# Routing of the second mixture beside its first expert products, mixture weights in transfers of 2 MB, and another order of the first transfers

## The chip, the cores and the metric

One core of a Trainium2 chip runs the whole program in one launch. The metric is device time in microseconds (us). Arrays are float32; some TensorE operands are in the type that the rows call fp32r, and a value is then carried as a high and a low part (names ending in h and l).

## The reference, cut to what matters

Two fused transformer blocks work on 256 tokens of width 1024. The first one has attention and a mixture of 32 experts (hidden width 512, two experts a token). The second one has two layers: a mixer each, then a dense feed-forward of width 2816 in the first layer and a mixture of 8 experts of that width, two a token, in the second, and a gated per-layer projection after each. This is the order of what is computed:

```python
x = x + ((g_gla * y_gla + g_att * y_att) @ w_out[l]).astype(x.dtype)      # first block
x = x + hier_moe(rms_norm(x, norm2_g[l]), w_router_group[l], ...)         # 32 experts
...
for i in range(DEPTH_2):                                                  # second block
    ...
    h = h + jnp.concatenate([y_a, y_b, y_c], axis=-1) @ w_out[i]
    hn = rms_norm_2(h, g_ffn[i])
    if i % 2 == 0:
        f = swiglu(hn, ffn_w1[j], ffn_w3[j], ffn_w2[j])
    else:
        f = moe_swiglu(hn, router_w[j], router_b[j], moe_w1[j], moe_w3[j], moe_w2[j])
    h = h + f
    gate = jax.nn.sigmoid(rms_norm_2(h, g_ple[i]) @ ple_gate_w[i])
    h = h + (p[i] @ ple_proj_w[i]) * gate
```

A mixture's expert computes `(silu(x @ w_gate[e]) * (x @ w_up[e])) @ w_down[e]` for the tokens that its router sends to it.

## The kernel before, in words

The phases run one after the other: b1 (the first block's attention), moe1 (the first mixture), mix0, ffn0, ple0, mix1, ffn1 (the second mixture, function `moe2`), ple1, and fin. Activations stay on the chip; weights are streamed.

**The stream (class `Stream`, lines 236 to 275).** `plan` (L525) lists all weight tiles of the program in the order of use, each [128, 2048] float32, 1 MB, or less. `fill` issues their loads on SP's queue (L264) as long as a buffer is free: one of three in the base ring, which any phase may use, or one of a wider pool that lives as long as its phase (`WIDE`, L23: 13 for moe1, 6 for ffn1). `get` hands out the next tile and frees the one handed out before. A phase's wide pool may be opened while the phase ahead still runs, and its loads start then.

**The start (`run`, L554).** x is loaded in two transfers on SP's queue, behind it the first three weight tiles; the vectors pv and the constants c0 come on ScalarE's queue, and the router table sm1 on GpSimd's. `block1` (L649) loads the constants c1, which the decay of the attention reads, and the smaller a2 on GpSimd's queue. The first products on TensorE are sums over the squares of x.

**The first mixture.** 128 tiles of gate and up weights (wgu) and 64 of down weights (wdn) come through the ring; the tokens of each expert are gathered by a product with a one-hot matrix.

**The second mixture (`moe2`, L1894).** The eight experts go in two halves c of four. In each half, 11 groups j make 256 hidden columns of the gate and up products: `first_products` (L1930) takes eight tiles k, and for each one calls `tiles` (L1918), which issues 16 matmuls with 32-column weights (two row blocks), copies three 512-column pieces of the tile to `fw` (picked by registers), and issues 12 matmuls from them for a third block, which is shared by the three fuller experts of four. The group's products are scaled by `rsl`, go through Silu and a multiplication into `ft`, and are transposed into `hT` beside the next group (`later`, `flush`). Then two times d of 22 tiles make the down products, evicted with the gate weights `wsl` into `ys`/`yf`, which `combine` sends back to the tokens by products with `pt`.

**Its routing.** In a pool m2r that is closed after the first group: logits, the two best experts (`top2`), the places of the tokens (`places`), the one-hot `P` (`base`: 64 places for each of four experts; `more`: 12 blocks of 32 further places, from the strips `px`), and the expert of each half that has fewest tokens (`fewest`). `gather(0)` makes the first half's inputs, eight gathers of 4 matmuls by column block, each two beside a tile of the first group. `of_slots` makes `rsl` by one-column sums. `rest()` is a generator with the remaining routing: the one-hot and the eight gathers of the second half, `of_slots` for it, the gate weights (`shares`), the transposes of P into `pt`, the products of P with the weights whose one-column sums make `wsl`, and the flag of the overflow. It is put into a queue at the first group's k = 3, and three of its steps are taken at each tile from there; what is left is drained after the group.

**The overflow.** If an expert has more tokens than places, a branch (`overflow`, L976) computes these again without limits. It stands behind group j = 5 of the first half, and its buffer xs lies in the last columns of hT.

**The order of the work.** The program is written in the order of the code, and a planner with costs of its own then orders the instructions of each engine; it does so for each stretch between branches by itself. Each engine and each queue then runs its list in order, and semaphores hold an instruction until its inputs are there.

## Time and profile before

| what | value |
|---|---|
| time, median of 3 runs | 2163.77 us (2163.45 to 2166.29) |
| the profiled execution | 2167.51 us, of which the span is 2165.9 us |
| granted TensorE clock, mean of the span | 0.976 |
| busy: PE, PEld | 2016.7 us (93%), 1461.7 us (67%) |
| busy: DVE, ACT, POOL | 1060.6 us (49%), 1080.2 us (50%), 18.7 us (1%) |
| DMA | 613.73 MB in 88665 packets, mean 283 GB/s |
| loads w<-wgu, w<-wdn, w<-m | 128, 64 and 264 of 1024 KB, 19.9, 19.9 and 10.7 us to landing |

PE is TensorE's matmuls, PEld its weight loads beside them, DVE VectorE, ACT ScalarE, POOL GpSimd, and SP issues loads alone. L230 is the one line that issues every matmul. A row names tiles as out<-in; in brackets stands the idle time before it and what ended it. The span in 40 slices of 54 us, each digit a tenth of the slice:

```profile
PE   7999998787877779999999999999899999999997
PEld 6999994222222248879999888866566756666746
PEclk9999999899999999999999999889999999999998
DMA  5344597999999983316555331449999999999981
```

The first mixture is in the slices 7 to 15, the second one in the slices 26 to 39.

### The profile page before, as it was taken

The numbers are of one execution on the slowest core, as the hardware profiler recorded it, in microseconds if no ns is written. First come the engines' busy times: TensorE is split into PE (matmuls) and PEld (weight loads), VectorE is DVE, ScalarE is ACT, GpSimd is POOL, SyncE is SP. The second block draws the span as 40 slices with busy tenths as digits, with TensorE's granted clock in tenths as the row PEclk, the third lists the DMA queues.
The fourth block names the chain that finished last, engine by engine and source line by source line (L and its number), as shares of the span: only waits on it lengthen the run. The fifth ranks groups of instructions, "written<-read, shape, count | busy, mean of one in ns | idle before, by whom it ended". The sixth has DMA issues, their size and how long they took to land. (4 is left out here: it accounts for less than half of the span.)

```text
span 2165.9 us, 44126 instructions
## 1 busy us (share of the span) xinstructions
PE 2016.7 (93%) x17740; PEld 1461.7 (67%) x17740; DVE 1060.6 (49%) x2809; ACT 1080.2 (50%) x2178; POOL 18.7 (1%) x29
## 2 busy tenths in 40 slices
PE   7999998787877779999999999999899999999997
PEld 6999994222222248879999888866566756666746
DVE  5787653100100037777666787536655115566115
ACT  5566642000000025456456735457677777777775
POOL 0000000000000010000000100000000000000000
PEclk9999999899999999999999999889999999999998
DMA  5344597999999983316555331449999999999981
GB/s 179 120 146 149 175 376 305 418 420 420 419 420 420 419 343 109 109 61 216 179 193 191 114 128 52 175 159 396 399 410 418 416 405 407 418 418 417 418 351 47
DMA packets 88665, 613.73 MB, mean 283 GB/s; under 512 B 9879, under 2 KB 12071, under 8 KB 18560
## 3 DMA queue, kind: packets, MB, share of 16 engines
q1 hardware_dynamic: 86272, 604.74, 71.1%
q0 software_dynamic: 1344, 5.10, 0.7%
q8 instruction: 143, 2.34, 0.4%
q10 hardware_dynamic: 832, 0.94, 0.1%
q14 instruction: 74, 0.61, 0.1%
HBM read 609.69 MB, written 1.05 MB: 282 GB/s over the span
## 5 line engine op out<-in xcount | busy, mean ns | idle before, releaser
L314 ACT COPY fw<-w 128x512 f32 x792 | 439.0, 617 | 137.3 <-ACT fw L314 91.9
L341 ACT CAST wh<-w 128x512 fp32r<-128x512 f32 (+2 forms) x500 | 289.8, 585 | 293.8 <-PE ps L230 247.1
L342 DVE TENSOR_TENSOR wl<-w,wh 128x512 fp32r<-128x512 f32 (+2 forms) x500 | 317.9, 646 | 169.9 <-ACT wh L341 161.8
L230 PE MATMUL ps<-w,hT 128*32 128x512 f32 x1920 | 311.0, 597 | 31.4 <-DMA w<-wdn 26.0
L230 PE MATMUL ps<-rawh,wh 128*128 128x256 f32 x960 | 277.4, 289 | 1.1 <-ACT rawh L341 1.1
L230 PE MATMUL ps<-rawl,wh 128*128 128x256 f32 x960 | 271.0, 282 | 0.5 <-DVE rawl L342 0.5
L230 PE MATMUL ps<-rawh,wl 128*128 128x256 f32 x960 | 270.5, 282 | 0.0
L230 PE MATMUL ps<-fw,xg 128*32 128x384 f32 (+2 forms) x2112 | 252.8, 382 | 0.0
L230 PE MATMUL ps<-w,xg 128*32 128x512 f32 x1024 | 199.5, 600 | 43.2 <-DMA w<-wgu 43.0
L2093 DVE STREAM_TRANSPOSE hT<-ft 32x64 f32<-32x64 f32 x968 | 228.3, 236 | 16.3 <-DVEq L985 0.7
L230 PE MATMUL ps<-w,rawh 128*32 128x512 f32 x1408 | 206.2, 607 | 6.4 <-issue 6.4
L230 PE MATMUL ps<-w,rawl 128*32 128x512 f32 x1408 | 211.7, 593 | 0.0
L230 PEld LDWEIGHTS ps<-w,hT 128*32 128x32 f32 x1920 | 116.8, 110 | 135.6 <-DMA w<-wdn 64.0
L230 PEld LDWEIGHTS ps<-fw,xg 128*32 128x32 f32 x2112 | 137.8, 110 | 83.0 <-issue 24.0
L230 PEld LDWEIGHTS ps<-rawh,wh 128*128 128x128 f32 x960 | 181.8, 190 | 5.1 <-ACT rawh L341 1.6
L230 PEld LDWEIGHTS ps<-rawl,wh 128*128 128x128 f32 x960 | 181.9, 190 | 1.9 <-DVE rawl L342 0.7
L230 PEld LDWEIGHTS ps<-rawh,wl 128*128 128x128 f32 x960 | 181.9, 189 | 1.5 <-issue 0.9
L230 PEld LDWEIGHTS ps<-w,xg 128*32 128x32 f32 x1024 | 42.1, 109 | 185.7 <-DMA w<-wgu 111.7
L230 PEld LDWEIGHTS ps<-w,rawl 128*32 128x32 f32 x1408 | 105.2, 110 | 34.4 <-issue 0.9
L230 PE MATMUL ps<-hh,wh 128*128 128x256 f32 x416 | 124.4, 300 | 0.1
L230 PE MATMUL ps<-fw,hT 128*32 128x128 f32 (+2 forms) x1056 | 121.1, 380 | 0.5 <-ACT fw L314 0.3
L230 PE MATMUL ps<-hh,wl 128*128 128x256 f32 x416 | 116.2, 281 | 0.2 <-DVE wl L342 0.2
(520 smaller groups left out, 2983.7 us busy)
## 6 DMA issues: line engine op xcount, KB each, us to landing
w<-m SPq DMA_DIRECT2D x264, 1024.0 KB, 10.7
w<-wgu SPq DMA_DIRECT2D x128, 1024.0 KB, 19.9
w<-wdn SPq DMA_DIRECT2D x64, 1024.0 KB, 19.9
w<-f SPq DMA_DIRECT2D x32, 1024.0 KB, 5.1
w<-wz SPq DMA_DIRECT2D x20, 1024.0 KB, 5.5
w<-wdh SPq DMA_DIRECT2D x24, 768.0 KB, 4.3
w<-wb SPq DMA_DIRECT2D x16, 1024.0 KB, 5.6
w<-wo SPq DMA_DIRECT2D x8, 1024.0 KB, 5.1
```

The source lines that it names most:

```text
L230: return self.k.nc.tensor.matmul(out, lhsT, rhs, start=new, stop=stop, skip_group_check=True, **kw)
L314: self.nc.scalar.copy(out, in_)
L341: self.nc.scalar.copy(h, src)
L342: self.nc.vector.tensor_sub(l, src, h.bitcast(F32))
L2093: nc.vector.transpose(hT[32 * f:32 * f + 32, 2 * j:2 * j + 2, o:o + 32], ts[r][32 * s:32 * s + 32, 64 * q:64 * q + 64].rearrange("p (i d) ...
```

## The change

It has three parts.

The mixtures' weights. Where the wide pool of moe1 or ffn1 has a free buffer, the stream loads two tiles by one transfer of 2 MB into a buffer [128, 4096] (6 such for moe1, 3 for ffn1). Where it has none, the pair goes into two free buffers of the base ring as two transfers of 1 MB. The host arrays m13 and m2 are laid out so that such a pair is one row of 16 KB in each partition.

```diff
-WIDE = {"b1": 0, "moe1": 13, "mix0": 0, "mix1": 0, "ffn0": 2, "ffn1": 6, "ple0": 4, "ple1": 4, "fin": 0}
+WIDE = {"b1": 0, "moe1": 6, "mix0": 0, "mix1": 0, "ffn0": 2, "ffn1": 3, "ple0": 4, "ple1": 4, "fin": 0}
...
-            c = [j for j in range(len(self.pools)) if self.free[j] and (j == 0 or ph == self.phase)]
-            if not c:
+            wide = len(self.pools) > 1 and self.free[1] and ph == self.phase
+            two = ph in ROUTED and not self.issued % 2
+            if two and wide:
+
+                self.free[1] -= 1
+                t = self.pools[1].tile([128, 4096], F32, name="w")
+                self.k.nc.sync.dma_start(t, self.whole[self.issued])
+                self.tiles += [(None, t[:, :2048]), (1, t[:, 2048:])]
+                self.issued += 2
+                continue
+            j = 1 if wide and ph not in ROUTED else 0
+            if self.free[j] < 1 + (two and j == 0):
                 return
-            j = c[-1]
             self.free[j] -= 1
             t = self.pools[j].tile([128, 2048], F32, name="w")
-            self.k.nc.sync.dma_start(t[:, :src.shape[-1]], src)
+
+            n = src.shape[-1] // (1 if self.issued else 4)
+            for c in range(0, src.shape[-1], n):
+                self.k.nc.sync.dma_start(t[:, c:c + n], src[:, c:c + n])
             self.tiles.append((j, t))
             self.issued += 1
...
-                    p += [(ph, A["m2"][c, i, k].rearrange("p e d -> p (e d)")) for i in range(2) for k in range(22)]
-        return p
+                    q += [A["m13"][c, j, k].rearrange("p k e d -> p (k e d)") for j in range(11) for k in range(4)]
+                    q += [A["m2"][c, i, k].rearrange("p k e d -> p (k e d)") for i in range(2) for k in range(11)]
+            for ap in q:
+                if ph in ROUTED:
+                    whole[len(p)] = ap
+                p += [(ph, h) for h in half(ap)]
+        return p, whole
```

The first transfers. x comes in four transfers, the program's first weight tile in four column pieces, and the constants c1 on SP's queue, behind what was issued on it before.

```diff
-            for k in range(0, 8, 4):
-                nc.sync.dma_start(x[:, k:k + 4], A["x"][k:k + 4].rearrange("k p s -> p k s"))
+            for k in range(0, 8, 2):
+                nc.sync.dma_start(x[:, k:k + 2], A["x"][k:k + 2].rearrange("k p s -> p k s"))
...
-            nc.gpsimd.dma_start(self.c1, self.A["c1"])
+            nc.sync.dma_start(self.c1, self.A["c1"])
```

The second mixture's routing. Its pool lies on the other side of the memory and stays open until the first half's groups are done. The fewest-token experts are found ahead of the one-hot, and of the further places only the first 96 of 384 columns are made ahead of the gather; the others follow at k = 5 of the first group, `of_slots` and `rest()` at k = 7. One step of `rest()` is then taken at each odd k of the following groups (`beside`), and what is left is drained after the eleven groups. The products of P with the gate weights go in two parts through a buffer of the pool tmp. The overflow's branch stands behind all groups of the first half, its buffer has a pool of its own, and the zeros of `yf` are written behind it; `ft` has three buffers in place of four.

```diff
+            right = lambda name: tc.tile_pool(reuse_waits="tile", name=name, bufs=1, side="right")
+            with ExitStack() as routing, tc.tile_pool(reuse_waits="tile", name="m2e", bufs=1) as work:
+                rt = routing.enter_context(right("m2r"))
...
-                def strips(src, name):
-
-                    s, o = four(src), rt.tile([128, 2, 2, 3, 4], F32, name=name)
-                    d = rt.tile([128, 2, 2, 3], F32, name=name + "d")
+                def thirds(src, name):
+
+                    s, d = four(src), rt.tile([128, 2, 2, 3], F32, name=name)
                     nc.vector.tensor_sub(d, s[:, :, :, 1:4], s[:, :, :, 0:3])
                     nc.vector.tensor_tensor(d, d, mk[:, None].to_broadcast([128, 2, 2, 3]), op=ALU.mult)
                     nc.vector.tensor_add(d, d, s[:, :, :, 0:3])
+                    return d
+
+                def strips(d, name):
+
+                    o = rt.tile([128, 2, 2, 3, 4], F32, name=name)
...
-                def more(c):
+                def more(c, places, a):
+
                     for t in range(2):
-                        nc.vector.tensor_tensor(v3(P[:, t, L * c + B:L * c + L], 32), bc(psx[:, t, c], 32),
-                                                iota[:, None, CAP2:CAP2 + 32].to_broadcast([128, 12, 32]), op=ALU.is_equal)
+                        o = v3(P[:, t, L * c + B + a:L * c + B + a + 32 * places.shape[-1]], 32)
+                        nc.vector.tensor_tensor(o, bc(places[:, t, c], 32), iota[:, None, CAP2:CAP2 + 32].to_broadcast(
+                            [128, places.shape[-1], 32]), op=ALU.is_equal)
...
+                    more(1, f["px"], 0)
+                    yield
                     yield from gather(1)
...
-                    wx = strips(Wt, "wx")
+                    wx = strips(thirds(Wt, "wd"), "wx")
...
-                            Pw = rt.tile([128, L], F32, name="Pw")
                             Pc = P[:, t, L * c:L * c + L].bitcast(F32)
-                            nc.vector.tensor_tensor(v3(Pw[:, :B], CAP2), v3(Pc[:, :B], CAP2), bc(Wt[:, t, 4 * c:4 * c + 4], CAP2),
-                                                    op=ALU.mult)
-                            nc.vector.tensor_tensor(v3(Pw[:, B:], 32), v3(Pc[:, B:], 32), bc(wx[:, t, c], 32), op=ALU.mult)
-                            for r in range(5):
-                                bw.mm(bw.t[:, 5 * c + r:5 * c + r + 1], Pw[:, 128 * r:128 * r + 128], self.cst("ones")[:, 0:1])
+                            for r0, n, col in ((0, CAP2, Wt[:, t, 4 * c:4 * c + 4]), (2, 32, wx[:, t, c])):
+                                m = n * col.shape[-1]
+                                Pw = self.tmp.tile([128, 512], F32, name="rsy")[:, :m]
+                                nc.vector.tensor_tensor(v3(Pw, n), v3(Pc[:, 128 * r0:128 * r0 + m], n), bc(col, n), op=ALU.mult)
+                                for r in range(m // 128):
+                                    bw.mm(bw.t[:, 5 * c + r0 + r:5 * c + r0 + r + 1], Pw[:, 128 * r:128 * r + 128],
+                                          self.cst("ones")[:, 0:1])
                             yield
...
+                fewest()
+                pst = thirds(ps, "pd")
                 base(0)
-                fewest()
-                psx = strips(ps, "px")
-                more(0)
+                more(0, pst, 0)
...
-                    if k == 2:
+                    if k == 5:
+                        f["px"] = strips(pst, "px")
+                        more(0, f["px"][:, :, :, 3:], 96)
+                    if k == 7:
                         self.of_slots(rsl[:, :5], P[:, :, :L], rs)
-                    if k == 3:
                         self.beside(rest(), late=True)
-                    for _ in range(3):
-                        self.tick()
-                g0 = first_products(0, during)
...
+                def beside(k):
+                    if k == 2:
+                        flush()
+                    if k % 2:
+                        self.tick()
...
                     for j in range(11):
-                        g = g0 if c == j == 0 else first_products(c, lambda k: flush() if k == 2 else None)
+                        g = first_products(c, beside if c or j else during)
                         ts = []
                         for r in range(3):
-                            t = work.tile([128, 256], F32, name="ft", bufs=4)
+                            t = work.tile([128, 256], F32, name="ft", bufs=3)
...
-                        if c == 0 and j == 5:
+                    if not c:
+                        self.drain()
+                        routing.close()
+
+                        with right("m2o") as room:
+                            xs = room.tile([128, 8, S], F32, name="xs")
                             self.overflow(pool, x, ("g_ffn1", xs, lambda: None), rk, *f["over"], E, units,
-                                          lambda i, k: m13[one(i[0]), one(i[1]), k, :, i[2]].rearrange("o u p d -> (o u p) d"),
-                                          lambda i, c, f: m2[one(i[0]), f, one(i[1]), c, :, i[2]].rearrange("o u p d -> (o u p) d"),
+                                          lambda i, k: m13[one(i[0]), one(i[1]), k // 2, :, k % 2, i[2]].rearrange("o u p d -> (o u p) d"),
+                                          lambda i, c, f: m2[one(i[0]), f, one(i[1]), :, c, i[2]].rearrange("o u p d -> (o u p) d"),
                                           lambda v: v.rearrange("p (q a i d) -> p q a i d", q=4, a=2, i=2))
+                        outs = routing.enter_context(right("m2y"))
+                        yf = [outs.tile([128, 512], F32R, name="yf" + n) for n in "hl"]
+                        for y in yf:
+                            nc.vector.tensor_scalar(y, iota[:, None, :].to_broadcast([128, 4, 128]), 0.0, None, op0=ALU.mult)
```

## Rows read from the trace of the kernel before

**Rows 1.** Stretches: us, busy (x) of PE, PEld, DVE, ACT, POOL; PEclk, DMA share, GB/s.

```profile
450.00:500.00 50.00, 40.19 (x190) 11.47 (x188) 5.04 (x9) 1.86 (x3) 0.00 (x0) 1.00 1.01 420
1500.00:1550.00 50.00, 50.00 (x597) 33.78 (x592) 32.72 (x133) 38.83 (x77) 0.00 (x0) 1.00 1.01 418
```

**Rows 2.** Waits: engine, tile, line, waited for; us in total, times, longest.

```profile
PE ps L230 <- DMA w<-wgu: 43.0, 71, 1.6
```

**Rows 3.** Waits of PE from 1460 to 2110 us.

```profile
PE ps L230 <- issue: 6.4, 1, 6.4
```

**Rows 4.** Timeline of PE from 1427 us: start, us, engine, line, operation, tiles.

```profile
1427.63 0.43 PE L230 MATMUL ps<-P,htmh 128*128 128x352 f32 x1
1427.90 0.32 PE L230 MATMUL ps<-P,html 128*128 128x352 f32 x1
...
1430.11 0.32 PE L230 MATMUL ps<-P,html 128*128 128x352 f32 x1
1430.37 1.92 PE L230 MATMUL ps<-w,rawh 128*32 128x512 f32 x16
1432.11 0.83 PE L230 MATMUL ps<-fw,xg 128*32 128x384 f32 x12
1432.87 0.43 PE L230 MATMUL ps<-P,htmh 128*128 128x352 f32 x1
```

**Rows 5.** Stretches in the second mixture.

```profile
1470.00:1550.00 80.00, 80.00 (x952) 52.91 (x945) 50.90 (x205) 61.19 (x122) 0.00 (x0) 1.00 1.01 405
1562.00:1660.00 98.00, 98.00 (x1126) 63.30 (x1120) 53.34 (x218) 70.32 (x139) 0.00 (x0) 0.99 0.99 404
1790.00:1990.00 200.00, 200.00 (x2299) 134.74 (x2295) 120.04 (x490) 149.00 (x295) 0.00 (x0) 1.00 1.01 415
```

**Rows 6.** DMA queues, 600 to 700 us: packets, MB, share of 16 engines.

```profile
q1 hardware_dynamic: 5761, 41.95, 101.2%
```

**Rows 7.** Timeline of PE at the start.

```profile
8.68 6.43 PE L230 MATMUL ps<-mt,c 128*128 128x256 f32 x16 [8.68 <-ACT mt L301]
15.29 0.50 PE L230 MATMUL ps<-wh,rawh 128*128 128x512 f32 x1 [0.18 <-ACT wh L341]
```

**Rows 8.** Timeline of ScalarE at the start.

```profile
1.40 0.53 ACTq L571 DMA_DIRECT2D c<-c  x1
...
7.80 0.30 ACT L341 CAST lrh<-sm 128x128 fp32r<-128x128 f32 x1 [4.56 <-DMA sm<-sm]
```

**Rows 9.** DMA issues of the page: tile, queue, KB, us to landing.

```profile
c<-c ACTq DMA_DIRECT2D x1, 337.0 KB, 6.2
```

**Rows 10.** Timeline of SP's queue ahead of the first mixture.

```profile
268.04 0.37 SPq L264 DMA_DIRECT2D w<-wgu  x1
...
300.68 16.14 SPq L264 DMA_DIRECT2D w<-wgu  x10
```

**Rows 11.** Stretches where the first mixture's transfers stop and go on.

```profile
330.00:335.00 5.00, 0.98 (x5) 0.57 (x3) 3.99 (x19) 1.28 (x3) 0.00 (x0) 0.84 0.06 26
...
340.00:345.00 5.00, 5.00 (x36) 1.84 (x38) 3.45 (x10) 0.47 (x1) 0.00 (x0) 0.81 0.23 36
```

**Rows 12.** DMA queues, 3 to 5 us.

```profile
q1 hardware_dynamic: 650, 0.65, 92.0%
```

**Rows 13.** Timeline of PE in the first mixture.

```profile
603.14 1.91 PE L230 MATMUL ps<-w,hT 128*32 128x512 f32 x8 [0.57 <-DMA w<-wdn]
```

**Rows 14.** Timeline of all engines ahead of the second mixture's first gather.

```profile
1408.08 0.15 DVE L1976 COPY px<-pxd 128x12 f32<-128x12 f32 x1
...
1408.44 0.16 DVE L1977 COPY px<-pxd 128x12 f32<-128x12 f32 x1
...
1408.66 1.95 DVE L1982 TENSOR_TENSOR P<-px,c 128x384 fp32r<-128x384 f32 x4
...
1409.34 0.63 PE L230 MATMUL ps<-P,htmh 128*128 128x352 f32 x1 [3.41 <-DVE P L1982]
```

**Rows 15.** Timeline of ScalarE: an activation table's load.

```profile
1457.35 1.28 ACT L303 ACT_TABLE_LOAD   x1
```

More of the change, by code (lines that the diff above doesn't have):

```diff
@@ L236, with __init__ @@
 class Stream:
-    def __init__(self, k, plan, base):
-        self.k, self.plan, self.i, self.issued, self.tiles = k, plan, 0, 0, []
+    def __init__(self, k, plan, whole, base):
+        self.k, self.plan, self.whole, self.i, self.issued, self.tiles = k, plan, whole, 0, 0, []
         self.pools, self.free, self.phase, self.last = [base], [RING], None, None
@@ L525, in plan @@
     def plan(self):
-        A, p = self.A, []
+        A, p, whole = self.A, [], {}
         half = lambda ap: [ap[:, i * (ap.shape[-1] // 2):(i + 1) * (ap.shape[-1] // 2)] for i in range(2)]
@@ L572, in run @@
             self.p = self.keep.tile([128, 2, S], F32, name="p")
-            self.W = Stream(self, self.plan(), ring)
+            self.W = Stream(self, *self.plan(), ring)
             self.W.fill()
@@ L1990, in rest @@
                         base(1)
-                    more(1)
+                    more(1, f["px"], 0)
+                    yield
                     yield from gather(1)
@@ L2040, in during @@
                         next(start, None)
-                    if k == 2:
+                    if k == 5:
+                        f["px"] = strips(pst, "px")
+                        more(0, f["px"][:, :, :, 3:], 96)
+                    if k == 7:
                         self.of_slots(rsl[:, :5], P[:, :, :L], rs)
-                    if k == 3:
                         self.beside(rest(), late=True)
-                    for _ in range(3):
-                        self.tick()
-                g0 = first_products(0, during)
-                self.drain()
-            m13 = self.A["m13"].rearrange("q j k p e d -> q j k p e d")
-            m2 = self.A["m2"].rearrange("q f (j c) p e d -> q f j c p e d", c=2)
-            def units(first, unit):
-                with tc.For_i(0, 2, 1) as q:
-                    first()
-                    with tc.For_i(0, 11, 1) as j:
-                        for e in range(4):
-                            unit((q, j, e), e)
-            one = lambda i: bass.ds(i, 1)
-            with tc.tile_pool(reuse_waits="tile", name="m2e", bufs=1) as work:
                 hT = work.tile([128, 22, R], F32, name="hT")
-                yf = [work.tile([128, 512], F32R, name="yf" + n) for n in "hl"]
-                for y in yf:
-                    nc.vector.tensor_scalar(y, iota[:, None, :].to_broadcast([128, 4, 128]), 0.0, None, op0=ALU.mult)
-                xs = hT[:, 16:].rearrange("p a r -> p (a r)")[:, :8 * S].rearrange("p (k s) -> p k s", k=8)
                 later = []
@@ L2070, in flush, with units @@
                         later.pop(0)()
+                def beside(k):
[3 more added lines that the diff above has]
+                        self.tick()
+                m13, m2 = self.A["m13"], self.A["m2"]
+                def units(first, unit):
+                    with tc.For_i(0, 2, 1) as q:
+                        first()
+                        with tc.For_i(0, 11, 1) as j:
+                            for e in range(4):
+                                unit((q, j, e), e)
+                one = lambda i: bass.ds(i, 1)
                 for c in range(2):
                     for j in range(11):
-                        g = g0 if c == j == 0 else first_products(c, lambda k: flush() if k == 2 else None)
+                        g = first_products(c, beside if c or j else during)
                         ts = []
                         for r in range(3):
-                            t = work.tile([128, 256], F32, name="ft", bufs=4)
+                            t = work.tile([128, 256], F32, name="ft", bufs=3)
                             gu = g[r].t.rearrange("p (q a d) -> p q a d", a=2, d=64)
@@ L2111, in moe2 @@
                                 flush()
-                        ys = [[work.tile([128, 512], F32R, name="y" + n, bufs=2) for n in "hl"] for _ in range(2)] + [yf]
+                        ys = [[outs.tile([128, 512], F32R, name="y" + n, bufs=2) for n in "hl"] for _ in range(2)] + [yf]
                         for r in range(3):
```

7 lines of the change are left out of this document (2 added, 5 removed).

## The prediction

> **What bounds the kernel now.** I read the stretches first (busy time, granted clock and DMA share side by side), then the waits, then the timelines of the three places that the change touches.
>
> The first mixture is bound by its transfers: the DMA engines are full at 420 GB/s while TensorE has gaps [rows 1], and what ends the gaps is a landing [rows 2]. The second mixture looks the same by its DMA share, also full, but TensorE has no gap there [rows 1]; from 1460 us to the stage's end it stood still once, for 6.4 us, at the overflow branch [rows 3]. So there the transfers follow TensorE, and only what TensorE executes, or waits for other than a landing, counts. A weight tile is 16 + 12 matmul records [rows 4]; 952 records in 80 us make 34 tiles, 2.35 us each [rows 5]. A tile's transfer takes 100 us / 40 = 2.50 us [rows 6]: the ring's lead melts by 0.15 us a tile and is refilled where TensorE evicts or branches, so neither side ever starves.
>
> **First transfers.** Now PE's first products (sums of squares) start at 8.68 and run 6.43 us, and the first weight product follows with no gap worth naming [rows 7]; so the start moves by what the sums move. ScalarE squares x just behind a cast that waited until 7.80 for the router table [rows 8]. The sums also need the constants on ScalarE's queue, which are issued at 1.40 [rows 8] and land 6.2 us later, so about 7.6 [rows 9]. Four x transfers instead of two, and the table of decay constants taken from GpSimd's queue to SP's behind x and three weight tiles, bring x forward, but not these constants: gain 8.68 - 7.6 = 1.1 at most for the sums, 0 at least if the cast stays first. More than that only if the clock rises sooner too; 2.5 is my far end. The four issues more on SP and the table's own wait are covered: its first reader (the decay products) comes some 20 us later than three tiles need at 420 GB/s. I take **-0.8** (0 to -2.5).
>
> **First mixture.** Two terms. (a) The ring ahead was 13 + 3 tiles; it becomes 6 double tiles and one pair in the base ring (a pair needs two free base slots of three), 14 MB. Sixteen transfers were issued before the stage began [rows 10], and then the DMA engines stood still from 331 to 344 because the ring was full and routing had not read anything [rows 11]. Two transfers fewer are ahead when reading starts, in a stage where every later microsecond belongs to the DMA: 2 x 2.50 = **+5.0**. (b) A row of 16 KB in place of 8 KB. An engine's time for a packet: 5761 packets, 41.95 MB (40 tiles, 5120 rows of 8 KB; the other 641 are 4-byte semaphore writes), in 101.2% of 16 x 100 us [rows 6] gives 316 ns for 8 KB; 650 packets of 1 KB (32 of them semaphore writes) in 92.0% of 16 x 2 us [rows 12] give 47.6 ns. A line through both: 37.4 ns per KB and 10 ns per packet. A 16 KB packet is then 622 ns instead of 632, 1.6% less; on the 178 transfers' worth still to come, 445 us, that is **-7.2**. Below, 0 if rows are cut at 8 KB as now; above, 10 ns may also shrink with the semaphore write saved, -8. The last step reads 2 MB where it read 1 MB, 1.9 us for eight matmul records now [rows 13], but sixteen in 1.92 us where both halves are there [rows 4]: 0 (0 to +1.9). Sum -2.2 (-4 to +7). The Trainium skill, DMA: Bandwidth & Descriptors, section Anatomy of one DMA, fits a transfer as about 2.0 us fixed plus bytes at 436 GB/s, and would make two 1 MiB transfers 8.8 us and one of 2 MiB 6.8, a quarter off the stage, some -100 us. The trace differs: these 40 transfers in 100 us [rows 6] show the fixed part already hidden by those in flight. The measurement decides.
>
> **Routing of the second mixture, its start.** TensorE waits 3.41 us for the one-hot of the first half [rows 14]. In front of that one-hot stand six small copies (0.07 us apart, 0.45) that move behind it, and its two blocks of 384 columns (0.49 each of 1.95 for four) shrink to 96, at least the 0.15 that a small operation takes [rows 14]: I take 0.2, so 0.3 less in front of the first product. **-0.8** (-0.3 to -1.6). The fewest-place arithmetic only changes order.
>
> **Routing spread.** The products of the routing are the same ones; in a stage that TensorE bounds, moving them saves nothing by itself, and the DMA idle time that vanishes was not on the path. What changes is how often the tile stream is broken. Gathers run on the whole array, tiles on 32-column bands. A tile alone takes 1430.37 to 1432.87, 2.50 us, against 2.35 in the stream; the sixteen gather matmuls before it take 1427.63 to 1430.37, 2.74, against 16 x 0.158 = 2.53 by their own step [rows 4]. So a break costs 0.15 + 0.20 = 0.35 us. Before: eight breaks, one after each of the first eight tiles (three routing steps in each). After: breaks before tiles 1, 2, 3 and 7 of group 0, then one routing step at every odd tile of the following groups: 8 gathers, 8 transposes, 4 weightings and the closing one, 21. 25 - 8 = 17 breaks more, **+5.9**. Bounds: 0 if the planner packs steps together; +8.7 if the weighting, now cut in two parts with a buffer of two, breaks the stream eight times more. The slow-clock stretch behind the one-column sums stays, twice as before. ScalarE gets a switch from Silu to Exp and back in the middle, 2 x 1.28 us by the load of now [rows 15]; its copies run one tile ahead and it has 0.7 us free per tile, so I count **+0.5** (0 to +1.5).
>
> **Overflow branch.** The 6.4 us [rows 3] are paid behind group 10 instead of group 5: 0 by itself. But the groups on its two sides differ: 2.35 us a tile before it, 1126 / 28 = 40.2 tiles in 98 us, 2.44, behind it, and 2299 / 28 = 82.1 in 200 us, 2.44, in the second half [rows 5]. The planner writes each stretch between branches by itself. Groups 6 to 10 now belong to the stretch ahead of the branch: 40 tiles x 0.083 = **-3.3** if they keep its order. Bounds: +3.3 if groups 1 to 5 take on the slow order, -10.6 if the second half takes on the fast one too (88 tiles more).
>
> The ring there is 8 MB instead of 9, in pairs. That costs nothing while TensorE is slower than the transfers over a group plus its evictions; I count 0 (0 to +3 at the end of the second half, where the lead is shortest).
>
> Sum: -0.8 - 2.2 - 0.8 + 5.9 + 0.5 - 3.3 = **-0.7 us**. The profiled execution took 2167.51 (span 2165.9), so 2166.8 by itself; the median shown is 3.7 lower, 2163.77, and the prediction is on that: **2163.1**.
>
> **Rivals.**
> - *The fast order spreads.* If the planner's order of group 1 to 5 also holds in the second half, -7.3 more: 2155.8. For it: transfers planned in 2 MB look shorter to the planner, and the slow groups begin where its first lead may have run out. Against: the branch still stands before the second half. Chance 0.26; fewer breaks or an earlier clock at the start would end near here as well.
> - *The 16 KB rows are no faster.* Then (b) goes and (a) stays: 2163.1 + 7.2 = 2170.3. For it: only two packet sizes carry the line, one of them mixed with another queue. Chance 0.11. It decides from a steady rate below 423 GB/s, where (a) outweighs (b).
> - *The clock falls in the first mixture.* Now a tile lands each 2.5 us and keeps TensorE 1.9 us, gaps 0.6 [rows 13]; landing in pairs and read four bands abreast it works 1.92 and waits 3.1. If the granted clock goes to 1.2 GHz there, the DMA hides it until the last landing; behind that stand the last tile pair (1.92 more) and the last combination and its evictions, some 3 us more: +5, 2168.1. The Trainium skill, TensorE: Matmul & The Clock Gate, section HAM oscillation, says that short work between waits for transfers lets the clock fall, and by it this rival would be the forecast; the trace has 1.00 in the stage [rows 1], with gaps of 0.6 only. Chance 0.11.
> - *The planned order goes slow in the first half.* Routing copies on ScalarE between the tile copies push groups 1 to 10 to 2.44: +6.6, 2169.7. Chance 0.10.
>
> **How the numbers follow.** The forecast has 0.42, its own range 2159.5 to 2167.5. What a measurement here tells from no change is 0.2%, 4.3 us: below 2159.5 or above 2168.1. Faster: 0.05 of the forecast, 0.25 of the first rival, 0.30. Slower: 0.01, then 0.10, 0.08 and 0.09 of the other rivals, 0.28. Same: 0.42. The range 2152 to 2173 takes in the first rival and the 16 KB one, and leaves about 0.1 on each side for two of them together.
>
> **What would show it.** The first weight product at 14 to 15 us, the table's landing well before its reader. DMA idle from 326 instead of 331; then 425 to 428 GB/s and a granted clock of 1.00 to the stage's end, which comes some 2 us earlier in its own length. The first gather 0.8 us sooner after the places. Twenty-odd breaks through groups 1 to 6, tiles between them at 2.50; groups 7 to 10 at 18.8 us; one idle piece of some 6 us between the first and second products. Wrong if TensorE is seen waiting for landings in the second mixture, or the stage changes by over 8 us.

## The result, and the profile after

The changed kernel took 2192.72 us in the median (2189.69 to 2195.13, 4 runs), the kernel before 2163.61 beside it: a ratio of 1.0131, 95% interval 1.0112 to 1.0150. Slower by 29 us; the range ended at 2173. The profiled execution took 2190.32 us (span 2188.7), 22.8 more than that of before; the one of before lies 3.9 above its median and this one 2.4 below, which makes 29 of the medians.

Where the time went can be read at a few landmarks of the two traces, in us:

| landmark | before | changed | changed minus before |
|---|---|---|---|
| first weight product | 15.29 | 12.61 | -2.7 |
| first mixture, first gather | 338.62 | 335.89 | -2.7 |
| first mixture, last down product ends | 792.62 | 787.73 | -4.9 |
| second mixture, first gather | 1409.34 | 1401.22 | -8.1 |
| second half's first copies | 1770.91 | 1767.66 | -3.3 |
| second mixture, last product ends | 2106.52 | 2129.30 | +22.8 |

So 8.1 us were won ahead of the second mixture (2.7 of them were there at 1382 us; much of the rest is the clock of these two executions, see the last section), 4.9 lost in its first half, and 26.0 in its second half. The stretches, in the columns of [rows 1] and [rows 5]:

```profile
450.00:500.00 50.00, 31.77 (x189) 10.57 (x189) 5.03 (x9) 1.86 (x3) 0.00 (x0) 0.83 1.01 426
...
1790.00:1990.00 200.00, 188.03 (x2073) 121.20 (x2067) 111.72 (x447) 135.15 (x265) 0.00 (x0) 1.00 0.97 385
```

The first mixture has 426 GB/s, 6 more than in [rows 1], and a granted clock of 0.83. In the second mixture 200 us hold 2073 matmul records where [rows 5] had 2299, and the DMA engines are no longer full (0.97, 385 GB/s). TensorE's waits there, in the columns of [rows 2], to be held against the one long wait of [rows 3] (three shorter ones in that view add up to 0.7 us):

```profile
PE ps L230 <- ACT fw L327: 16.4, 25, 1.1
PE ps L230 <- DVEq L1001: 12.3, 1, 12.3
```

One wait more has 1.8 us (ScalarE's yfh). There is no landing among them: TensorE waits for ScalarE's copies (fw), and at the branch for VectorE's queue. (The second mixture's weights came in 99 transfers of 2 MB and 66 of 1 MB, the latter through the base ring.)

**The boundary of two groups.** In the second half a group of eight tiles takes 21.76 us from its first copy to the next group's, before 19.55. All of it lies at the boundary and just behind it; the tiles after that take 2.36 us in both. Eviction means here the scaling with Silu on ScalarE and the multiplication on VectorE that take a group's products out of ps into ft. ScalarE's timeline of before at one such boundary:

```profile
1892.58 0.47 ACT L303 ACTIVATE ft<-ps,rsl 128x256 f32<-128x256 f32 x1 [1.48 <-PE ps L230]
1893.44 0.47 ACT L303 ACTIVATE ft<-ps,rsl 128x256 f32<-128x256 f32 x1 [0.38 <-PE ps L230]
1894.12 0.31 ACT L303 ACTIVATE ft<-ps,rsl 128x64 f32<-128x64 f32 x1 [0.20 <-PE ps L230]
1894.33 0.61 ACT L314 COPY fw<-w 128x512 f32 x1
1894.84 0.32 ACT L303 ACTIVATE ft<-ps,rsl 128x64 f32<-128x64 f32 x1
1895.05 1.13 ACT L314 COPY fw<-w 128x512 f32 x2
1896.61 0.31 ACT L303 ACTIVATE ft<-ps,rsl 128x64 f32<-128x64 f32 x1 [0.43 <-DVE ft L2083]
1896.82 1.12 ACT L314 COPY fw<-w 128x512 f32 x2
```

The two evictions of 128x256 are the blocks r = 0 and 1; the three of 128x64 belong to the third block. The copies of the next group's first tile stand between them. In the changed kernel:

```profile
1900.53 0.47 ACT L316 ACTIVATE ft<-ps,rsl 128x256 f32<-128x256 f32 x1 [1.47 <-PE ps L230]
1901.38 0.47 ACT L316 ACTIVATE ft<-ps,rsl 128x256 f32<-128x256 f32 x1 [0.38 <-PE ps L230]
1902.06 0.31 ACT L316 ACTIVATE ft<-ps,rsl 128x64 f32<-128x64 f32 x1 [0.20 <-PE ps L230]
1903.67 0.31 ACT L316 ACTIVATE ft<-ps,rsl 128x64 f32<-128x64 f32 x1 [1.29 <-DVE ft L2108]
1903.88 0.61 ACT L327 COPY fw<-w 128x512 f32 x1
1905.00 0.31 ACT L316 ACTIVATE ft<-ps,rsl 128x64 f32<-128x64 f32 x1 [0.51 <-DVE ft L2108]
1905.21 1.12 ACT L327 COPY fw<-w 128x512 f32 x2
```

Four evictions come ahead of the first copy, and the fourth and fifth wait 1.29 and 0.51 us for VectorE's multiplication (L2108) of the piece before. VectorE in the same stretch:

```profile
1902.83 0.48 DVE L2118 STREAM_TRANSPOSE hT<-ft 32x64 f32<-32x64 f32 x2
1903.35 0.28 DVE L2108 SCALAR_TENSOR_TENSOR ft<-ps,rsl,ft 128x64 f32<-128x64 f32 x1
1903.66 0.98 DVE L2118 STREAM_TRANSPOSE hT<-ft 32x64 f32<-32x64 f32 x4
1904.68 0.28 DVE L2108 SCALAR_TENSOR_TENSOR ft<-ps,rsl,ft 128x64 f32<-128x64 f32 x1
```

Each multiplication stands behind transposes of the blocks just finished (2 to 4 of some 0.25 us). So the copies come late, and TensorE's products on them with them:

```profile
1904.54 0.83 PE L230 MATMUL ps<-fw,xg 128*32 128x384 f32 x4 [0.83 <-ACT fw L327]
```

The same kernel's groups j = 7 to 10 of the first half took 18.9 us: there the planner wrote copy and eviction in turn.

**The branch.** TensorE stands for 12.28 us at it; VectorE had all 44 transposes of the last group ahead of its own branch instruction (first TensorE, then the last 28 of them on VectorE):

```profile
1654.35 3.48 PE L230 MATMUL ps<-w,hT 128*32 128x512 f32 x16 [12.28 <-DVEq L1001]
```

```profile
1647.07 6.97 DVE L2118 STREAM_TRANSPOSE hT<-ft 32x64 f32<-32x64 f32 x28
```

In the kernel before, 16 of the 44 stood ahead of VectorE's branch and 28 behind it:

```profile
1559.08 7.00 DVE L2093 STREAM_TRANSPOSE hT<-ft 32x64 f32<-32x64 f32 x28 [0.67 <-DVEq L985]
```

### The profile page after: what moved, and what is told of

Same layout as the page of the kernel before. It is cut to its first block, busy times and chain, and to the rows that moved or that the text cites. A ratio compares the mean times of both kernels' runs of the same rounds, so it can differ in the third digit from the quotient of the medians.

```text
span 2188.7 us, 43808 instructions
## 1 busy us (share of the span) xinstructions
PE 1963.6 (90%) x17740; PEld 1408.1 (64%) x17740; DVE 1065.5 (49%) x2811; ACT 1085.7 (50%) x2180; POOL 18.1 (1%) x28
## 3 DMA queue, kind: packets, MB, share of 16 engines
q8 instruction: 144, 2.36, 0.4%
## 5 line engine op out<-in xcount | busy, mean ns | idle before, releaser
L230 PE MATMUL ps<-w,hT 128*32 128x512 f32 x1920 | 285.5, 653 | 55.0 <-DMA w<-wdn 40.0
L230 PE MATMUL ps<-w,xg 128*32 128x512 f32 x1024 | 159.9, 715 | 87.7 <-DMA w<-wgu 87.7
L230 PE MATMUL ps<-fw,xg 128*32 128x384 f32 (+2 forms) x2112 | 210.2, 381 | 13.3 <-ACT fw L327 13.3
L230 PEld LDWEIGHTS ps<-w,hT 128*32 128x32 f32 x1920 | 102.5, 116 | 151.2 <-issue 67.8
L230 PEld LDWEIGHTS ps<-fw,xg 128*32 128x32 f32 x2112 | 122.9, 110 | 112.2 <-ACT fw L327 47.7
L230 PE MATMUL ps<-w,rawh 128*32 128x512 f32 x1408 | 171.4, 597 | 0.0
L230 PEld LDWEIGHTS ps<-w,xg 128*32 128x32 f32 x1024 | 33.1, 121 | 198.6 <-DMA w<-wgu 137.2
L230 PE MATMUL ps<-hl,wh 128*128 128x256 f32 x416 | 115.8, 279 | 0.0
```

What stands on the lines that cost most here:

```text
L230: return self.k.nc.tensor.matmul(out, lhsT, rhs, start=new, stop=stop, skip_group_check=True, **kw)
```

## The experiments

Twelve kernels were run. The times were taken on several chips, so each is given as the ratio to the kernel before on the same chip. "Stage" is the time from the second mixture's first gather to the end of its last weight product in the profiled execution; it leaves out what happens ahead. The first group alone takes 39.5 to 42.7 us in the six kernels that keep the routing of before (before, e6, e7, e8, e10, e11), so a difference of under 3 us between their stages tells nothing. A group is read from its first copy's start to the next group's.

| kernel | ratio (95%) | stage | groups j = 7 to 9, first half | groups j = 2 to 9, second half | idle at branch |
|---|---|---|---|---|---|
| before | 1 | 697.2 | 19.55 | 19.55 | 6.4 |
| changed | 1.0131 (1.0112-1.0150) | 728.1 | 18.9 | 21.76 | 12.3 |
| e1 changed, 1 MB | 1.0008 (0.9991-1.0025) | 703.1 | 19.55 | 19.55 | 12.4 |
| e12 the same, 8 tiles | 1.0008 (0.9990-1.0027) | 704.6 | 19.55 | 19.55 | 12.4 |
| e2 changed, evictions later | 1.0239 (1.0217-1.0261) | 754.2 | 18.9 | 23.4-25.4 | 12.3 |
| e3 changed, transposes later | 1.0043 (1.0028-1.0058) | 711.7 | 18.9 | 20.22 | 13.5 |
| e5 changed, both later | 1.0033 (1.0020-1.0045) | 706.9 | 18.9 | 18.93, then 19.7-20.3 | 15.0 |
| e4 changed, branch at 8 | 1.0093 (1.0070-1.0116) | 727.9 | (branch) | 21.76 | 12.3 |
| e9 the same, held | 1.0108 (1.0086-1.0131) | 723.1 | (branch) | 21.76 | 6.6 |
| e6 before, ffn1 in 2 MB | 1.0218 (1.0201-1.0235) | 745.4 | 23.4-23.8 | 21.76 | 6.3 |
| e7 before, start and moe1 | 0.9975 (0.9964-0.9985) | 695.9 | 19.55 | 19.55 | 6.6 |
| e8 e7, both later | 0.9956 (0.9940-0.9973) | 696.0 | 19.56 | 19.56 | 6.5 |
| e10 e8, ffn1 in 2 MB | 1.0028 (1.0015-1.0042) | 706.2 | 18.9 | 18.93, then 19.7-20.2 | 13.6 |
| e11 e10, held | 1.0001 (0.9986-1.0016) | 698.5 | 18.9 | 18.93, then 19.7-20.9 | 6.9 |

**e1: the second mixture in 1 MB again.** Three lines of the changed kernel:

```diff
-WIDE = {"b1": 0, "moe1": 6, "mix0": 0, "mix1": 0, "ffn0": 2, "ffn1": 3, "ple0": 4, "ple1": 4, "fin": 0}
+WIDE = {"b1": 0, "moe1": 6, "mix0": 0, "mix1": 0, "ffn0": 2, "ffn1": 6, "ple0": 4, "ple1": 4, "fin": 0}
...
-            two = ph in ROUTED and not self.issued % 2
+            two = ph == "moe1" and not self.issued % 2
...
-            j = 1 if wide and ph not in ROUTED else 0
+            j = 1 if wide and ph != "moe1" else 0
```

> The changed kernel, but the second mixture's weights come in 1 MB transfers again (six wide buffers of one tile); the first mixture keeps its 2 MB. Theory A (the order of ScalarE's list): with 1 MB transfers the planner writes the third block's evictions and the next tile's copies in turn (eviction, eviction, eviction, copy, eviction, two copies, eviction), so a group of eight tiles in the second half goes from 21.76 to 19.55 us, 11 x 2.2 = 24 us less; groups 7 to 10 of the first half lose the order that they had, 18.93 to 19.55, about 3 us more: 2192.7 - 21 = about 2171. Theory B (2 MB transfers free and fill the ring too coarsely, so tiles land late): also faster, about 2168, and the first half stays at 18.9 a group. Theory C (routing spread or the three ft buffers slow the second half): stays at about 2192, groups at 21.8.

Measured 1.0008, with 19.55 us a group in both halves, and in the second half ScalarE's list as before at each boundary. From its first copy to its end the second half takes 335.8 us, 361.6 in the changed kernel and 335.6 before: the pairs alone cost 25.8 us there. This rules theory C out; A and B stay.

**e2: the third block's evictions behind the next tile's copies.** The pieces of r = 2 are put into a list and written when the next group has issued its first tile:

```diff
+                def thirdly():
+                    with self.after(self.copied):
+                        while third:
+                            third.pop(0)()
...
+                    if k == 1:
+                        thirdly()
...
+                            if r < 2:
+                                evict([(slice(0, 4), r)])
+                            else:
+                                third.append(lambda evict=evict: evict([(slice(b, b + 1), 2 + of_block[b]) for b in range(3)]))
```

> The changed kernel with its 2 MB transfers untouched; only the evictions of a group's third block are written behind the copies of the next group's first tile. Theory A (order): a group of the second half goes to 18.9 to 19.3 us, 11 x 2.6 = 29 us less, about 2164, with the DMA engines full again (over 410 GB/s) there. Theory B (late landings of 2 MB): nothing changes, groups stay at 21.8 us and ScalarE's copies wait for landings instead, 2190 or more. Theory C (routing spread): nothing changes.

It went the other way, 1.0239. The first tile's three copies did come first, but ScalarE's list then has the evictions between the second tile's copies, and these wait for VectorE up to 4.02 us:

```profile
1911.88 0.31 ACT L316 ACTIVATE ft<-ps,rsl 128x64 f32<-128x64 f32 x1
1912.09 1.13 ACT L1941 COPY fw<-w 128x512 f32 x2
1917.24 0.31 ACT L316 ACTIVATE ft<-ps,rsl 128x64 f32<-128x64 f32 x1 [4.02 <-DVE ft L2117]
```

```profile
1911.41 5.48 DVE L2131 STREAM_TRANSPOSE hT<-ft 32x64 f32<-32x64 f32 x22
```

22 transposes stand ahead of the multiplication that the eviction waits for. So theory A in its plain form (the place of the evictions) is wrong as well; what costs is an eviction that waits, with copies queued behind it.

**e3: the transposes behind the multiplications.**

```diff
-                                nc.vector.scalar_tensor_tensor(t4[:, q], gu[:, q, 1], u, t4[:, q], op0=ALU.mult, op1=ALU.mult)
+                                last = nc.vector.scalar_tensor_tensor(t4[:, q], gu[:, q, 1], u, t4[:, q], op0=ALU.mult, op1=ALU.mult)
...
-                        def post(j=j, ts=ts):
-
+                        def post(j=j, ts=ts, last=(nc.cur_bb, last)):
+
+                          with self.after(last):
```

> The changed kernel with its 2 MB transfers and with the same order on ScalarE in the second half; only VectorE's transposes of a group are held behind the group's last multiplication. Theory A, in its finer form (ScalarE waits 1.3 and 0.5 us a group for multiplications that stand behind transposes on VectorE): these two waits shrink to about 0.3 together, a group goes to about 20.3 us, 11 x 1.5 = 16 us less, about 2177. If it is ScalarE's order alone that costs (four evictions of 0.3 to 0.5 us ahead of the copies), under 5 us are gained. Theory B and C: no change.

Measured 20.22 us a group and 1.0043, as theory A's finer form had it. ScalarE's list is the one of the changed kernel, and its waits for VectorE are 0.35 and, at the fifth eviction, none:

```profile
1900.88 0.32 ACT L316 ACTIVATE ft<-ps,rsl 128x64 f32<-128x64 f32 x1 [0.20 <-PE ps L230]
1901.55 0.31 ACT L316 ACTIVATE ft<-ps,rsl 128x64 f32<-128x64 f32 x1 [0.35 <-DVE ft L2108]
1901.76 0.61 ACT L327 COPY fw<-w 128x512 f32 x1
```

**e5: both.**

> The changed kernel with its 2 MB transfers and its routing; both orders of the runs before are put together: the third block's evictions behind the copies of the next group's first tile, and VectorE's transposes behind the group's last multiplication. If ScalarE's copies lose time only because they are queued behind evictions that wait for multiplications that stand behind transposes, a group of the second half takes 18.9 to 19.2 us, 11 x 2.7 = 30 us less than in the changed kernel, about 2163 (as fast as the kernel before, 1.000), and the DMA engines are full there at 2 MB a transfer. If 2 MB transfers through eight buffers are themselves a limit, groups stay above 19.8 us and TensorE or ScalarE waits for landings.

For five groups 18.93 us. Then 19.7 to 20.3 us, with the DMA engines full and landings to wait for:

```profile
1800.00:1870.00 70.00, 70.00 (x830) 45.47 (x825) 46.80 (x192) 54.05 (x110) 0.00 (x0) 1.00 1.01 418
1890.00:1990.00 100.00, 97.50 (x1127) 49.14 (x1123) 60.57 (x245) 71.92 (x146) 0.00 (x0) 1.00 1.01 423
```

```profile
ACT fw L1941 <- DMA w<-m: 27.4, 15, 3.2
```

So 2 MB transfers through eight tiles don't hold the second half at 21.76: its order on two engines did. With that mended, the transfers are the next limit, 8 x 2.48 us a group at 423 GB/s. The total, 1.0033, is not the 1.000 that I expected: the branch's idle time grew to 15.0 us, since the 44 transposes ahead of VectorE's branch now start only behind the group's last multiplication.

**e6: 2 MB in the second mixture alone, on the kernel before.**

> The kernel before with one part of the change alone: the second mixture's weights in 2 MB transfers (three wide buffers of two tiles), the first mixture and the routing as before. The planner's list for ScalarE has all five evictions ahead of the next tile's copies from group 5 of the first half on, and four of five in the second half. Theory A (order): groups of 21.8 us or more in the second half (+24 us) and in groups 6 to 10 of the first half (+2.2 to 3 each, +12): about 2200, 1.017. Theory B (late landings of 2 MB transfers by themselves): the first half's groups stay at 18.9 us, as they were in the changed kernel with the same transfers, and the total is about 2188. Theory C (routing spread is the cause): no change from before, 2163.

1.0218: this one part costs more by itself than the whole change. In the first half the groups take 23.4 to 23.8 us, where the changed kernel with the same transfers took 18.9: the transfers are the same, the planner's list is not (all five evictions ahead of the copies here).

**e12: 1 MB transfers with a ring of eight tiles** (five wide buffers in e1's place of six).

> The changed kernel with the second mixture's weights in 1 MB transfers and five wide buffers, so that eight tiles fit as with the 2 MB transfers (the first run of 1 MB had nine). If the size of a transfer makes the planner's order, the order is that of the first run and groups of the second half stay at 19.55 us, the total near 1.001 of before. If the shorter ring (8 tiles in place of 9) is what costs, waits for landings appear and groups go towards 20 to 21.8 us, 1.004 or more.

1.0008 and 19.55 us again: it is the pairs that turn the list, and not the ring's 8 MB. A pair is two things, a transfer of 2 MB and one buffer that two tiles share; no run tells them apart.

**e4 and e9: the branch.** In e4 the block with the branch stands inside the loop over j, at `c == 0 and j == 8`.

> The changed kernel with the overflow branch behind the ninth group of the first half (j = 8) in place of the eleventh. TensorE's idle 12.3 us at the branch, in which VectorE runs the last group's transposes, should fall to the 6.4 us of the kernel before, as the next group's products don't read them: 2192.7 - 6 = about 2187, with the second half at 21.8 us a group as before it. Rival: the idle time is the branch's own and comes along, 2192.

The idle time stayed at 12.3 us: the rival, so far. In e9 one VectorE write more, which needs x as the branch leaves it, holds the group's transposes behind the branch:

```diff
+ nc.vector.tensor_scalar(hT[:, 16:18], x[:, 0:2, 0:1].to_broadcast([128, 2, R]), 0.0, None, op0=ALU.mult)
```

> The run with the branch behind the ninth group, and one VectorE write more (a value of x times zero over the two columns of hT that the ninth group fills later), which holds that group's 44 transposes behind the branch. Theory: TensorE stands at the branch until VectorE's list has come to it, and the list had the 44 transposes ahead (44 x 0.25 = 11 us). Then the idle time at the branch falls from 12.3 to 4 us or less and the time by 7 to 8 us, about 2181. Rival: the branch costs every engine its own load of the flag and refill (6.3 us were seen on the sequencer), and the idle time stays at 6 to 12 us.

6.63 us idle and a stage shorter by 4.8 us; the total doesn't show it (1.0108 against e4's 1.0093, intervals that overlap), so the 7 to 8 us that I expected of it are not there. All engines around the branch (the transposes go on to the end of the window):

```profile
1612.80 9.24 DVE L2118 STREAM_TRANSPOSE hT<-ft 32x64 f32<-32x64 f32 x37
...
1615.10 3.64 PE L230 MATMUL ps<-w,rawh 128*32 128x512 f32 x16 [6.63 <-issue]
```

Both sides had a part. What is the branch's own can be read on the sequencers (PEldq is TensorE's; durations in ns: shortest, median and longest of two instructions, of which one is the branch over the overflow's code):

```profile
L1001 PEldq COMPARE_BRANCH  x2: 75/3116/6156, 1606.5 to 1608.7; - x2
L1001 DVEq COMPARE_BRANCH  x2: 47/54/61, 1610.9 to 1611.1; - x2
```

TensorE's branch instruction takes 6.16 us, VectorE's 0.06 at most. In the changed kernel TensorE's took 6.38 us, from 1642.27 to 1648.65; what came on top, until 1654, was VectorE's list. On one chip e11 against e10, which differ by such a write alone (over the columns 10 and 11), shows it in the time too: 13.6 to 6.9 us idle, 1.0028 to 1.0001 (the intervals just meet).

**e7, e8, e10, e11: which parts are worth keeping.** e7 is the kernel before with the new start and the first mixture in 2 MB.

> The kernel before with two other parts of the change: the first transfers' order, and the first mixture's weights in 2 MB transfers. By the changed kernel's trace: 1.8 us from the start, 2 us from the first mixture's rate of 425 GB/s, 1.5 us given back behind it at a lower granted clock: 2163.6 - 2.3 = about 2161, 0.999. If the fall of the clock in the first mixture costs more than its transfers gain, 2164 or more.

0.9975, faster than both kernels.

> The kernel of the run before (start and first mixture as changed, second mixture in 1 MB and routing as before) with both orders, evictions and transposes later. If the order on ScalarE and VectorE is what a group's time hangs on, with 1 MB transfers too, groups 6 to 10 of the first half and all groups of the second half go from 19.55 to 18.9 us: 16 x 0.6 = 10 us less, about 2151, 0.994. If the stream of 1 MB transfers is the limit there (2.50 us a tile, 20 us a group), nothing is gained: 2161.

The ratio is 0.9956, but the stage is no shorter than e7's (696.0 and 695.9) and a group takes 19.56 us: the 10 us that I expected of the orders are not there. e8's profiled execution had its first gather 11.1 us earlier than e7's, in code that is the same (the clock, below); the intervals of the two overlap. Nor is the list the one that the expectation was made for. With 1 MB transfers the same edit puts the three evictions together, ahead of all copies of the second tile, and two of them wait for VectorE:

```profile
1881.05 1.65 ACT L1941 COPY fw<-w 128x512 f32 x3
1882.60 0.32 ACT L316 ACTIVATE ft<-ps,rsl 128x64 f32<-128x64 f32 x1
1883.26 0.31 ACT L316 ACTIVATE ft<-ps,rsl 128x64 f32<-128x64 f32 x1 [0.35 <-DVE ft L2106]
1883.93 0.31 ACT L316 ACTIVATE ft<-ps,rsl 128x64 f32<-128x64 f32 x1 [0.35 <-DVE ft L2106]
```

In e5 and e10 the planner wrote copy and eviction in turn there, and a group took 18.93 us. In e8's second half nothing waits for a landing. So e8 doesn't show that 1 MB transfers are the limit; that order with 1 MB transfers was not run.

> The first transfers and both mixtures' 2 MB transfers as in the change, routing and branch as in the kernel before (behind group j = 5), and both orders (evictions and transposes later). If what the changed kernel lost is the order, the routing's spread and the branch, this takes the rest: groups of the first half at 18.9 us, of the second at 18.9 until the ring's lead is gone and then 19.8 (DMA full at 423 GB/s): 4 x 0.6 + 5 x 0.6 us below the run with 1 MB transfers (0.9956), about 2152 or 0.993. If 2 MB transfers cost something else in the second mixture, no better than 0.9956.

> The run before with the sixth group's 44 transposes held behind the branch by one VectorE write, as in the run with the branch at the ninth group. If VectorE's list sets the idle time of TensorE at the branch, it falls from 6 us to 4 or less: another 2 to 3 us, about 2149, 0.992. If not, the same as the run before.

Both missed: the groups took 18.9 us until the lead was gone, and then waited for landings. With the order mended and the branch's list held, 2 MB transfers in the second mixture give 1.0001, more than the 0.9956 of e8 with 1 MB; the stage less its first group is 659.0 against 653.5 us.

## Why the prediction was wrong

**The step that failed** is the last one of "Overflow branch": "The ring there is 8 MB instead of 9, in pairs. That costs nothing while TensorE is slower than the transfers over a group plus its evictions; I count 0 (0 to +3 at the end of the second half, where the lead is shortest)." It measured +26.0 us in the second half, 25.8 of them by the pairs alone (e1). I looked at the pairs as transfers and asked when they land. They did land in time. But they are an input of the planner too: with them it wrote four evictions ahead of the copies for the whole second half (e1 and e12 against the changed kernel), and ScalarE's and VectorE's lists then wait for each other at every boundary (e3, e5). I had named the planner's two orders and a price of 0.08 us a tile; for the second half I allowed only the faster one (-7.3), and a slow order beyond the known one not at all. Why the planner's list turns on the pairs is not shown by these runs.

**The first rival could not be.** A faster order in the second half was to give 7.3 us more. e10 and e11 had that order, and after four or five groups the transfers held them at 19.7 us or more. The 19.55 us a group of the kernel before are already less than eight transfers of 2.50 us take; the ring's lead paid the difference. The eleven groups of the second half together took 221.0 and 221.4 us in e10 and e11, 221.2 before: the lead was used up sooner, and nothing was won. (e5 had 219.9.) "Only what TensorE executes, or waits for other than a landing, counts" held for an order that leaves the DMA engines full; it doesn't say that there is something to win.

**First transfers**, -0.8: -2.7 at the first weight product, of which 1.8 stay from 50 us on. The sums start at 5.72 and not at 7.6:

```profile
5.72 4.39 PE L230 MATMUL ps<-mt,c 128*128 128x256 f32 x12 [5.72 <-DMA c<-c]
...
12.61 0.50 PE L230 MATMUL ps<-wh,rawh 128*128 128x512 f32 x1 [0.54 <-ACT wh L354]
```

```profile
c<-c ACTq DMA_DIRECT2D x1, 337.0 KB, 4.2
```

I had bounded the constants by the old landing of 6.2 us [rows 9]; with the table gone from GpSimd's queue and x in smaller pieces they land after 4.2. A landing time read beside other traffic is no property of the transfer. The 1.8 that stay are inside my range to -2.5; the 2.7 at first are not. The cast for the router table, whose place in front was to give my 0, went behind the squares in ScalarE's list.

**First mixture**, -2.2: from its first gather to its last down product 454.0 us became 451.8, -2.2. The rate:

```profile
q1 hardware_dynamic: 3354, 42.53, 100.5%
```

100.5% of 16 x 100 us for 42.53 MB, 425 GB/s against 420 [rows 6], 1.4% more. The packets of the two traces bear the cause out: one of 8 KB took 315 ns, one of 16 KB 617, 2% less than two of 8 KB. That the sum agrees to 0.1 us is luck, as both of its terms were too large. Fifteen tiles were ahead when the stage began to read, not fourteen (six transfers of 2 MB and three of 1 MB), so the first is +2.5 by its own price. And 1.4% of 445 us are 6.2 and not 7.2: of the stage's 96 pairs 83 came as one transfer and 13 as two of 1 MB, through the base ring. These two would make -3.7. The Trainium skill (DMA: Bandwidth & Descriptors, Anatomy of one DMA) gives a transfer a fixed part of about 2.0 us, there for those that GpSimd issues; these are issued on SP's queue, and 109 transfers in place of 192 brought 1.4%, not a quarter.

**The clock in the first mixture** fell as the rival had it:

```profile
599.33 3.62 PE L230 MATMUL ps<-w,hT 128*32 128x512 f32 x16 [2.98 <-DMA w<-wdn]
604.23 1.92 PE L230 MATMUL ps<-w,hT 128*32 128x512 f32 x16 [1.28 <-DMA w<-wdn]
```

The gaps are 1.3 and 3.0 us where they were 0.6 [rows 13], the same sixteen records take 1.92 us or 3.62, and the granted clock of the stretch from 450 to 500 us is 0.83 against 1.00 [rows 1]. That agrees with the Trainium skill, TensorE: Matmul & The Clock Gate, HAM oscillation. Its price was small, as the DMA hides it: of the 4.9 us won at the stage's end 3.4 are left at 961 us, by a cast of the same weight piece in both traces; at most 1.5 were given back (the rival said 5). Even these aren't shown to be its price: the granted clock from 800 to 900 us, 0.97 and 1.00 before and 0.93 changed, is 0.93 to 1.00 in the other executions of the same code there (e7, e8, e10, e11).

**Start of the routing**, -0.8: the wait for the one-hot is 2.53 us instead of 3.41, -0.9:

```profile
1401.22 0.63 PE L230 MATMUL ps<-P,htmh 128*128 128x352 f32 x1 [2.53 <-DVE P L2006]
```

**Routing spread and order of groups 6 to 10**, +5.9 + 0.5 - 3.3 = +3.1: in the first half the stage lost 4.9 us, of which the branch's idle time is 5.9; the rest is -1.0, some 4 us less than forecast. The breaks and the order were not measured apart. The groups behind the routing kept the fast order, 18.9 us, as said.

**The branch**, 0: +5.9. I moved it without asking what each engine has ahead of it in its list; behind group 10 as behind group 8 it was 44 transposes, 11 us (e4, e9), where behind group 5 it had been 16. It was the place in VectorE's list, not in the code, that counted.

## What to carry to other kernels

Where a planner writes the lists, a change of the transfers can change every engine's order: compare the lists at one boundary of the steady loop before looking at bytes. A short eviction that waits on another engine costs all that is queued behind it, so work that nobody waits for soon (transposes here) belongs behind the chain of eviction and multiplication. The same edit to the order can come out as another list when the transfers differ (e8, e10). And of a bundle of edits, here three, the parts are worth running singly: the start and the first mixture gave 0.9975, the rest took 1.6% away.

## What was not expected of the hardware

In e7, e8, e10 and e11 the instructions ahead of the second mixture's first gather are the same, and in the same order on TensorE, ScalarE and VectorE, and it starts at 1408.2, 1397.1, 1403.3 and 1404.4 us, by how long the granted clock stays at its lower level (0.50, 1.2 GHz) in a few places. One place are the one-column sums ahead of that gather. In the kernel before, TensorE was busy all the time there, and the clock was (columns as above):

```profile
1380.00:1385.00 5.00, 5.00 (x44) 4.88 (x43) 1.38 (x2) 1.26 (x2) 0.00 (x0) 1.00 0.50 198
1385.00:1390.00 5.00, 5.00 (x31) 5.00 (x30) 0.69 (x1) 0.63 (x1) 0.00 (x0) 0.64 0.00 0
...
1395.00:1400.00 5.00, 5.00 (x25) 5.00 (x26) 1.73 (x11) 1.64 (x5) 0.00 (x0) 0.50 1.03 434
```

In e8 the stretch from 1380 to 1385 had 1.00 and the next 0.66, with the routing's first waits in it already; in e7 every stretch from 1385 to the gather had 0.50. Of the 11.1 us between the two, 5.5 came at the sums and 5.2 were there before, 3.0 of these between 1299 and 1310 us, where the clock was 0.71 in e7 and 1.00 in e8. Of the 8.1 us that the changed kernel had won at its gather, 5.4 came behind 1382 us; 0.9 of them are the shorter wait, and most of the rest is of this kind. TensorE's branch over the overflow's code took 5.9 to 6.4 us on its sequencer in the second mixture of every kernel, and TensorE stood 6.3 to 6.9 us at it where no list held it up longer.
